# Attention steps and output-projection weight loads at other places among a projection's products

## The chip, the cores and the metric

The kernel runs on one core of one Trainium2 chip. The metric is the device time of one execution, in microseconds (us); the time of a kernel is the median over its runs.

## What is computed

One layer of a hybrid encoder on 512 tokens of width 1024. All 16 attention heads are fed by one input projection, and all are gathered by one output projection into the residual. A gated MLP with a short convolution and a gated per-layer embedding follow; the change does not touch these.

```
hn = rms_norm(h, ln_mix);  z = hn @ w_in
q1, q2, k1, k2, va, qf, kf, vf, fg, qc, kc, vc = split(z)     # all q, k: RMS norm per head
o_a = diff_attention(...)        # A: 4 heads, softmax(q1 k1) - lam * softmax(q2 k2), then a norm
o_b = forgetting_attention(...)  # B: 6 heads, bias from a cumulative log forget gate, causal
o_c = chunk_attention(...)       # C: 6 heads, bias by clipped relative position, causal by chunk
h = h + concat([o_a, o_b, o_c]) @ w_out
h = h + conv_gated_mlp(rms_norm(h, ln_ffn), ...)
h = h + (p @ w_ple_proj) * sigmoid(rms_norm(h, ln_ple) @ w_ple_gate)
```

## The kernel before

Heads are worked on in eight pairs: A0, A1, B0, B1, B2, C0, C1, C2, with two heads (0 and 1) in each. The 512 tokens are four tiles of 128. To keep float32 accuracy, every operand of a product is split into a rounded part `hi` and the rest `lo`, and a product is three matmuls (`mm3`, hi*hi, hi*lo, lo*hi).

The input projection runs part by part (`PARTS`: A0, A0b, A1, A1b, B0, B1, B2, C0, C1, C2; A has two sets of queries and keys, so `A1b` is A1's second). Each part has four units, one for each token tile: `in_unit` accumulates eight steps of three matmuls in a PSUM bank `z` (two buffers) and then evicts it: values `V`, sums of squares `sq` on ACT, their reduction `rs` on DVE, a power on POOL, and the scaled queries and keys `zn` on DVE, after which the bank is free. Each such unit is a slot; slots 4 to 39 are these units, 40 to 47 the units of the output projection's first pass (`out_unit`, names `wo`): two column halves of four token tiles, six steps of three matmuls, over pairs 0 to 5. The second pass, `last_out`, adds pairs 6 and 7 (C1 and C2) when C2 is done and is followed by the FFN.

The attention is cut into steps, generators that are run in between the product steps of a slot:

- `a`, `b` (`qk_cols`): transposes of the queries and keys and their splits; POOL moves the halves to their places (tiles `q_q`, `k_k`, `kl`).
- `s...` (`scores`): for each query tile two matmuls into a bank `s` (two buffers), on DVE the bias and the row's extreme in one instruction that evicts the bank (`CUSTOM_DVE_ANT_0` in the profile), the exponential on ACT, a reciprocal on DVE, the scaling on POOL. In A the second set (`A_1b_s` and the like) is subtracted from the first on DVE.
- `p0`, `p1` (`prob_cols`): transposes of head 0's and head 1's probabilities (`pt`, `ptc`) and their splits.
- `v0`, `v1` (`values`): probabilities times values into the bank `o`, evicted into `oall`.
- `n` (`subln`): A's norm; `fc`: the cumulative gate.

`T` gives for each step a slot and the product step in it from which it may run; `run` takes one attention step after each product step and runs what is left over, in a row, when the slot's products are through. With that TensorE's order is written out by hand. The order on ACT, DVE and POOL is chosen at build time by a planner, and `EARLY` raises a step's priority there. SP's queue issues most DMAs.

Weights are loaded into staging tiles (`_r`, four buffers); ACT copies `hi`, and `lo = raw - hi` is made in one of three ways, chosen by `lo_by` from a pair of counts `"w" + part`: `(a, b)` gives the last `a` of the loads to an accumulating DMA (ACT writes `-raw` rounded into `lo`, and a DMA issued on POOL's queue adds `raw`), the `b` before them to POOL, and the rest to DVE. `wO0` and `wO1` are the output projection's pairs 0 to 5 for the two column halves, `wO6` the four loads of pairs 6 and 7, in the order (6,0), (6,1), (7,0), (7,1). Split weights lie in rings of eight tiles.

Nearly all instructions carry L78 in the profile, the line of the helper that records them, so they are told apart by tile names, with the pair's number left out: `A1b_z` are A1b's products, `C_s` scores of any C pair, `wo` products of the output projection, `wo_l` its `lo` weights, `n_t` and `u` the FFN.

Of the kernel before, what the change touches and what calls it, by code (L numbers as in the profile page):

```python
# [53 lines left out]
def kernel(ctx: ExitStack, tc: tile.TileContext, x, xt0, xt, pt_in, small, g_ffn_in, bias_c,  # L54
# [636 lines left out]
    def at(slot, gen, *args, start=1, early=0):  # L691
        steps.setdefault(slot, []).append((start, early, gen, args))
# [8 lines left out]
    def run(fill, todo):  # L701
# [18 lines left out]

    T = {
# [13 lines left out]
    }  # L735
    EARLY = {"C1s1": 80, "B1v0": 20, "C0s1": 20, "C1p0": 20, "B0p0": 10, "A0b": 10, "B1p1": 20, "A1b": 10,
# [5 lines left out]

    def add(key, gen, *args):
        at(T[key][0], gen, *args, start=T[key][1], early=EARLY.get(key, 0))

# [999 lines left out]
```

## Time and profile before

| | |
|---|---|
| median of 3 runs | 728.63 us (727.79 to 728.96) |
| profiled execution | 727.37 us, span 725.6 us |
| granted TensorE clock, mean | 0.999 |
| TensorE busy | 705.8 us (97%) |
| VectorE (DVE) busy | 556.3 us (77%) |
| ScalarE (ACT) busy | 394.1 us (54%) |
| GpSimd (POOL) busy | 267.3 us (37%) |

The span is that of the trace, from the first to the last instruction; the execution's own time has a little around it. A line of the timeline has a start and a duration in us, the engine, the source line, the operation and its tiles (output <- inputs), and in brackets the idle time before it and what ended that. Matmuls overlap their neighbours, so the distance from one start to the next is what each takes of TensorE.

### The profile page before, as it was taken

The numbers are of one execution on the slowest core, as the hardware profiler recorded it, in microseconds if no ns is written. First come the engines' busy times: TensorE is split into PE (matmuls) and PEld (weight loads), VectorE is DVE, ScalarE is ACT, GpSimd is POOL, SyncE is SP. The second block draws the span as 40 slices with busy tenths as digits, with TensorE's granted clock in tenths as the row PEclk, the third lists the DMA queues.
The fourth block names the chain that finished last, engine by engine and source line by source line (L and its number), as shares of the span: only waits on it lengthen the run. The fifth ranks groups of instructions, "written<-read, shape, count | busy, mean of one in ns | idle before, by whom it ended". The sixth has DMA issues, their size and how long they took to land. (4 is left out here: it accounts for less than half of the span.)

```text
span 725.6 us, 11877 instructions
## 1 busy us (share of the span) xinstructions
PE 705.8 (97%) x4218; PEld 632.3 (87%) x4218; DVE 556.3 (77%) x1091; ACT 394.1 (54%) x745; POOL 267.3 (37%) x355
## 2 busy tenths in 40 slices
PE   9998999999999999999999999999999999999997
PEld 8888989898999887889888899888998888899886
DVE  7678788887878855758879968787898779988552
ACT  6656775865766664565555544543444543544821
POOL 5676676756665640211101144031520004361400
PEclk9999999999999999999999999999999999999999
DMA  9454425514211135564545334552263322122531
GB/s 330 170 139 110 124 59 124 138 30 110 88 53 52 59 66 167 170 208 90 144 138 125 101 97 122 142 156 66 88 178 114 95 87 83 57 73 93 159 126 58
DMA packets 36950, 83.22 MB, mean 115 GB/s; under 512 B 4214, under 2 KB 6262, under 8 KB 36892
## 3 DMA queue, kind: packets, MB, share of 16 engines
q1 hardware_dynamic: 32844, 73.52, 32.4%
q0 software_dynamic: 3760, 8.66, 6.4%
q8 instruction: 33, 0.54, 0.3%
q10 hardware_dynamic: 288, 0.30, 0.1%
q14 instruction: 25, 0.20, 0.1%
HBM read 74.19 MB, written 4.21 MB: 108 GB/s over the span
## 5 line engine op out<-in xcount | busy, mean ns | idle before, releaser
L78 DVE TENSOR_TENSOR w_lo<-w_raw,w_hi 128x768 fp32r<-128x768 f32 (+1 forms) x118 | 114.4, 989 | 20.2 <-ACT w_hi L78 19.6
L78 ACT CAST w_hi<-w_raw 128x768 fp32r<-128x768 f32 (+1 forms) x118 | 89.6, 786 | 70.1 <-POOL w_raw L78 32.0
L78 PE MATMUL u<-Tl,w_hi 128*128 128x512 f32 (+1 forms) x336 | 125.5, 374 | 0.8 <-DVE Tl L78 0.8
L78 PE MATMUL u<-Th,w_hi 128*128 128x512 f32 (+1 forms) x336 | 125.6, 374 | 0.6 <-ACT pps L78 0.6
L78 PE MATMUL u<-Th,w_lo 128*128 128x512 f32 (+1 forms) x336 | 125.3, 373 | 0.0
L78 POOL TENSOR_TENSOR w_raw<-w_raw,w_raw 128x768 f32<-128x768 f32 (+1 forms) x30 | 54.3, 1833 | 145.2 <-DVE w_lo L78 113.8
L78 PEld LDWEIGHTS u<-Tl,w_hi 128*128 128x128 f32 x336 | 63.0, 188 | 13.1 <-DVE Tl L78 1.2
L78 PEld LDWEIGHTS u<-Th,w_hi 128*128 128x128 f32 x336 | 63.0, 188 | 12.9 <-ACT pps L78 1.0
L78 PEld LDWEIGHTS u<-Th,w_lo 128*128 128x128 f32 x336 | 63.0, 188 | 12.5
L78 DVE SCALAR_TENSOR_TENSOR c<-u,cols,c 128x511 f32<-128x511 f32 x76 | 56.6, 746 | 18.6 <-ACT c L78 17.4
L78 POOL DMA_DIRECT2D w_raw<-in_w_up_dram x9 | 7.9, 907 | 100.1 <-DMA w_raw<-in_w_up_dram 93.9
L78 ACT ACTIVATE c<-u,cols 128x512 f32<-128x512 f32 x38 | 29.5, 776 | 22.7 <-PE u L78 22.7
L78 PE MATMUL dn_X<-w_hi,g_ah 128*128 128x256 f32 x144 | 40.7, 282 | 0.3 <-DVE h L78 0.3
L78 PE MATMUL dn_X<-w_lo,g_ah 128*128 128x256 f32 x144 | 40.6, 282 | 0.3 <-DVE w_lo L78 0.3
L78 PE MATMUL dn_X<-w_hi,g_al 128*128 128x256 f32 x144 | 40.5, 281 | 0.0
L78 PE MATMUL B_z<-B_h,Th 128*128 128x384 f32 x96 | 34.5, 360 | 0.6 <-DVE B_zn L78 0.6
L78 PE MATMUL C_z<-C_h,Th 128*128 128x384 f32 x96 | 34.3, 357 | 0.0
L78 PE MATMUL B_z<-B_h,Tl 128*128 128x384 f32 x96 | 32.3, 337 | 0.0
L78 PE MATMUL B_z<-B_l,Th 128*128 128x384 f32 x96 | 32.3, 337 | 0.0
L78 PE MATMUL C_z<-C_h,Tl 128*128 128x384 f32 x96 | 32.3, 336 | 0.0
L78 PE MATMUL C_z<-C_l,Th 128*128 128x384 f32 x96 | 32.3, 336 | 0.0
L78 PEld LDWEIGHTS dn_X<-w_hi,g_ah 128*128 128x128 f32 x144 | 27.1, 188 | 0.9 <-ACT w_hi L78 0.5
(484 smaller groups left out, 2143.8 us busy)
## 6 DMA issues: line engine op xcount, KB each, us to landing
w_raw<-in_w_up_dram SPq DMA_DIRECT2D x50, 384.0 KB, 3.9
w_raw<-in_w_down_dram SPq DMA_DIRECT2D x24, 384.0 KB, 3.1
w_raw<-in_w_up_dram SPq DMA_DIRECT2D x22, 256.0 KB, 3.3
B_r<-in_w_in_dram SPq DMA_DIRECT2D x12, 384.0 KB, 3.1
C_r<-in_w_in_dram SPq DMA_DIRECT2D x12, 384.0 KB, 3.3
wo_r<-in_w_out_dram SPq DMA_DIRECT2D x16, 256.0 KB, 3.0
w_raw<-in_w_ple_gate_dram SPq DMA_DIRECT2D x16, 256.0 KB, 3.0
h<-in_x_dram SPq DMA_DIRECT2D x4, 512.0 KB, 7.7
```

Source lines behind the costliest of these rows:

```text
L78: ins = getattr(self.eng, op)(*a, **k)
```

## The change

Both tables are changed: `T` (places of steps, and the counts for three sets of weights that are used: `wB0a`, and `wO0`, `wO1`, `wO6`) and `EARLY`. On TensorE these steps move: A0's second-head scores, two product steps later, so that the last three follow their slot's products in a row; B0's query and key transposes and A1's first values and second transposes, one or two product steps later; C0's second-head scores and first transposes, one or two earlier; C1's steps one to three later; and C2's scores, transposes and values, by 2 to 8 us later in TensorE's order, the four scores of its second head in a row behind the output tile of slot 43. The last of B0's four `lo` parts goes from an accumulating DMA to DVE. In the output projection, `lo` of pair 5, first half, goes from DVE to POOL; of pairs 0 and 1, second half, from POOL to DVE; of pairs 2 to 5, second half, from accumulating DMAs to POOL; of pair 6, second half, from DVE to POOL; of pair 7 from DVE and POOL to accumulating DMAs.

```diff
     T = {
         "A0a": (6, 2), "A0b": (9, 4), "fc": (11, 0), "A1a": (16, 4), "A1b": (17, 0), "A0s01": (10, 4),
-        "A0s02": (10, 5), "A0p0": (12, 3), "A0s11": (13, 0), "A0v0": (12, 5), "A0s12": (13, 1), "A0p1": (15, 5),
-        "A0v1": (16, 7), "A0n": (17, 0), "A1s01": (18, 2), "A1s02": (18, 5), "A1p0": (20, 5), "A1s11": (20, 6),
-        "A1v0": (22, 6), "A1s12": (21, 3), "A1p1": (23, 1), "A1v1": (24, 7), "A1n": (27, 7), "B0a": (22, 2),
-        "B0s0": (24, 1), "B0s1": (24, 1), "B0p0": (25, 0), "B0v0": (25, 1), "B0p1": (26, 0), "B0v1": (26, 2),
+        "A0s02": (10, 7), "A0p0": (12, 3), "A0s11": (13, 2), "A0v0": (12, 5), "A0s12": (13, 5), "A0p1": (15, 5),
+        "A0v1": (16, 7), "A0n": (17, 1), "A1s01": (18, 2), "A1s02": (18, 4), "A1p0": (20, 5), "A1s11": (20, 6),
+        "A1v0": (23, 0), "A1s12": (21, 3), "A1p1": (23, 1), "A1v1": (24, 5), "A1n": (27, 7), "B0a": (22, 3),
+        "B0s0": (24, 1), "B0s1": (24, 1), "B0p0": (25, 0), "B0v0": (25, 0), "B0p1": (26, 0), "B0v1": (26, 1),
         "B1a": (24, 1), "B1s0": (25, 4), "B1s1": (26, 0), "B1p0": (26, 7), "B1v0": (28, 3), "B1p1": (29, 0),
         "B1v1": (29, 3), "B2a": (28, 4), "B2s0": (29, 4), "B2s1": (30, 4), "B2p0": (30, 6), "B2v0": (32, 0),
-        "B2p1": (32, 1), "B2v1": (33, 3), "C0a": (32, 3), "C0s0": (33, 4), "C0s1": (34, 1), "C0p0": (34, 7),
-        "C0v0": (35, 7), "C0p1": (36, 0), "C0v1": (36, 5), "C1a": (36, 0), "C1s0": (37, 3), "C1s1": (38, 4),
-        "C1p0": (38, 5), "C1v0": (40, 0), "C1p1": (40, 2), "C1v1": (41, 0), "C2a": (40, 3), "C2s0": (41, 3),
-        "C2s1": (42, 0), "C2p0": (42, 1), "C2v0": (43, 7), "C2p1": (44, 0), "C2v1": (45, 4), "wA0b": (4, 2),
-        "wA1a": (0, 0), "wA1b": (1, 0), "wB0a": (1, 0), "wB1a": (2, 0), "wB2a": (2, 0), "wC0a": (1, 1),
-        "wC1a": (1, 1), "wC2a": (0, 1), "wO0": (0, 0), "wO1": (4, 4), "wO6": (0, 1),
+        "B2p1": (32, 1), "B2v1": (33, 3), "C0a": (32, 2), "C0s0": (33, 3), "C0s1": (34, 0), "C0p0": (34, 5),
+        "C0v0": (35, 7), "C0p1": (36, 0), "C0v1": (36, 5), "C1a": (36, 1), "C1s0": (37, 4), "C1s1": (38, 5),
+        "C1p0": (39, 0), "C1v0": (40, 1), "C1p1": (40, 3), "C1v1": (41, 2), "C2a": (40, 3), "C2s0": (42, 2),
+        "C2s1": (43, 7), "C2p0": (43, 7), "C2v0": (44, 3), "C2p1": (44, 7), "C2v1": (46, 3), "wA0b": (0, 2),
+        "wA1a": (0, 0), "wA1b": (1, 0), "wB0a": (0, 0), "wB1a": (2, 0), "wB2a": (2, 0), "wC0a": (1, 1),
+        "wC1a": (1, 1), "wC2a": (0, 1), "wO0": (0, 1), "wO1": (0, 4), "wO6": (2, 1),
     }
...
```

In `EARLY`, `B1v0`, `C0v1`, `B1v1`, `C0s0`, `A0p0` and `B1a` lose their priority, `B0v0` goes from 40 to 10, `C1v1` from 40 to 10, `C1s0` from 40 to 20, and new are `C2v1` 10, `C2v0` 80, `A0s02` 20, `C0v0` 40, `B0s0` 20, `B0p1` 20, `B2v1` 80, `fc` 80 and `C2p0` 80.

More of the change, by code (lines that the diff above doesn't have):

```diff
@@ L722 @@
         "A0a": (6, 2), "A0b": (9, 4), "fc": (11, 0), "A1a": (16, 4), "A1b": (17, 0), "A0s01": (10, 4),
[4 rows of a table removed]
[4 rows of a table added]
         "B1a": (24, 1), "B1s0": (25, 4), "B1s1": (26, 0), "B1p0": (26, 7), "B1v0": (28, 3), "B1p1": (29, 0),
         "B1v1": (29, 3), "B2a": (28, 4), "B2s0": (29, 4), "B2s1": (30, 4), "B2p0": (30, 6), "B2v0": (32, 0),
[6 rows of a table removed]
-    }
-    EARLY = {"C1s1": 80, "B1v0": 20, "C0s1": 20, "C1p0": 20, "B0p0": 10, "A0b": 10, "B1p1": 20, "A1b": 10,
[5 rows of a table removed]
[6 rows of a table added]
+    }
+    EARLY = {"C1s1": 80, "C0s1": 20, "C1p0": 20, "B0p0": 10, "A0b": 10, "B1p1": 20, "A1b": 10, "A1v1": 80,
[5 rows of a table added]
     def add(key, gen, *args):
```

10 rows, old and new, of the table EARLY are left out of this document.

## The prediction

> **What bounds the kernel now.** I read the page first, then TensorE's own waits, then its timeline round each wait, and only then the other engines there.
>
> ```profile
> span 725.6 us, 11877 instructions
> PE 705.8 (97%) x4218; PEld 632.3 (87%) x4218; DVE 556.3 (77%) x1091; ACT 394.1 (54%) x745; POOL 267.3 (37%) x355
> ```
>
> TensorE is busy for 97% of the span. The change adds and removes none of its 4218 products; it only puts some of them elsewhere in its order. The time can therefore move only by TensorE's waits. The columns of the next view are: who waited for whom, us in total, times, longest.
>
> ```profile
> PE A1b_z L78 <- DVE A1b_zn L78: 1.0, 1, 1.0
> PE wo L78 <- DMA wo_l<-wo_r: 0.9, 1, 0.9
> PE C_s L78 <- POOL C_k_k L398: 0.4, 1, 0.4
> ```
>
> I set the PE orders of both programs side by side, step by step. Up to the first scores of A0's second head they are the same, and after the last output product as well. Between them, steps move in four places. The first and the last hold these three waits, so they are all that the change can win. Of the other waits none stands where a step moves. The timeline gives their true size, since a product's end overlaps the next one's start and only distances between starts count:
>
> ```profile
> 76.40 0.28 PE L78 MATMUL A1b_z<-A1b_l,Th 128*128 128x256 f32 x1
> 76.52 0.28 PE L78 MATMUL A1b_z<-A1b_h,Tl 128*128 128x256 f32 x1
> 77.78 0.36 PE L78 MATMUL A1b_z<-A1b_h,Th 128*128 128x256 f32 x1 [0.98 <-DVE A1b_zn L78]
> 252.65 0.39 PE L78 MATMUL wo<-wo_h,Tl 128*128 128x512 f32 x1
> 253.43 0.38 PE L78 MATMUL C_s<-C_k_k,C_q_q 128*128 128x256 f32 x1 [0.40 <-POOL C_k_k L398]
> 272.62 0.39 PE L78 MATMUL wo<-wo_h,Tl 128*128 128x512 f32 x1
> 272.85 0.40 PE L78 MATMUL wo<-wo_h,Th 128*128 128x512 f32 x1
> 274.14 0.50 PE L78 MATMUL wo<-wo_l,Th 128*128 128x512 f32 x1 [0.89 <-DMA wo_l<-wo_r]
> 274.48 0.40 PE L78 MATMUL wo<-wo_h,Tl 128*128 128x512 f32 x1
> ```
>
> A 256-wide product takes 0.12 (76.40 to 76.52) and a 512-wide one 0.23 (272.62 to 272.85). So the first wait costs 1.26 - 0.12 = 1.14, the second 0.78 - 0.23 = 0.55, the third 1.29 - 0.23 = 1.06. The product that resumes is itself followed late (274.14 to 274.48 is 0.34, not 0.23), 0.11 more each time. In all 3.1 us, 0.4% of the time, is the most that can come back.
>
> **A0's second head.** Its scores come two product steps later among A1b's products; the last three now stand in a row behind A1b's second tile. That tile is complete sooner, and the chain that frees its bank is put forward on ACT, DVE and POOL:
>
> ```profile
> 73.19 0.69 DVE L78 CUSTOM_DVE_ANT_0 A_e<-A_s,bias_A 128x512 f32<-128x512 f32 x1
> 74.27 0.67 DVE L78 CUSTOM_DVE_ANT_0 A_3b_e<-A_3b_s,bias_A 128x512 f32<-128x512 f32 x1
> 74.87 0.42 DVE L78 TENSOR_REDUCE A1b_rs<-A1b_sq 128x4 f32<-128x256 f32 x1
> 76.09 1.02 POOL L383 TENSOR_TENSOR A1b_rs<-A1b_rs,nhalf 128x4 f32<-128x4 f32 x1
> 77.15 0.48 DVE L78 SCALAR_TENSOR_TENSOR A1b_zn<-A1b_z,rstd,A1b_rs 128x256 f32<-128x256 f32 x1 [1.15 <-POOL A1b_rs L383]
> ```
>
> Before, the reduce (74.87) stands behind both 512-wide score evictions; after, ahead of them. About 0.8 us earlier it carries its power (1.02) and the scaling (0.48) with it, and the 1.14 + 0.11 wait is covered. But there are only two score banks, and three scores in a row need them at the rate of DVE: an eviction of 0.69, 0.2 longer than two products of 0.23, and its hand-over make TensorE wait an estimated 0.3, twice, with 0.11 each to resume: 0.8. Two more things are added on DVE. The subtraction for B0's last weights, until now an accumulating DMA, and A1b's third scaling, which goes behind two subtractions of B1's weights:
>
> ```profile
> L78 DVE TENSOR_TENSOR B_l<-B_r,B_h x7: 937/950/1399, 59.0 to 106.8; 128x768 fp32r<-128x768 f32 x7
> ```
>
> The first lands where DVE idles before the transposed probabilities are evicted, so of its 0.95 I count next to nothing. The second frees a bank that B0's first tile wants; it is held 2 x 0.95 longer, of which by my reckoning all but 0.4 passes before TensorE comes there. This place sums to -1.25 + 0.8 + 0.4 = -0.05. Ends: -1.25 (no new wait) and +0.6 (the old wait stays half).
>
> **B0, A1, C0 and C1.** These steps move by one product step of B or C (three products) to three of the output projection; A1's second-head eviction and C0's first transposes move with them. In the stretch of the first of them TensorE waits for nothing:
>
> ```profile
> 121.00:132.00 11.00, 11.00 (x72) 10.73 (x71) 9.04 (x18) 7.51 (x15) 8.31 (x12) 1.00 0.23 61
> ```
>
> (Columns: stretch, its length, busy time of PE, PEld, DVE, ACT, POOL, granted clock, DMA share, GB/s.) There is nothing to win; DVE has 2 of 11 us free as cover; without it a step would lose its 0.3 to 0.5 us shift. I take 0, with 0 and +0.5 as ends. `wA0b` is never asked for, as A0's weights are loaded without that table.
>
> **C2 and the output projection's weights.** C2's first scores go 3.5 us later, so the key moves on POOL that held them up are done: -0.55 - 0.11. The `lo` halves of weights 2 to 5 of the second column half come from POOL instead of accumulating DMAs, so the 1.06 + 0.11 wait goes, if POOL is in time.
>
> ```profile
> 241.92 3.05 POOL L149 TENSOR_TENSOR wo_l<-wo_r,wo_h 128x512 fp32r<-128x512 f32 x2 [1.75 <-ACT wo_h L78]
> 253.00:284.40 31.40, 30.11 (x150) 24.74 (x150) 14.96 (x41) 15.57 (x36) 8.08 (x13) 1.00 0.37 86
> ```
>
> Four subtractions of 1.5 us fit well into a POOL that is busy for 8 of 31 us, and ACT loses four negated copies. What two of these cost on POOL earlier, at 241.92, goes to DVE, and one of the first half's goes to POOL in its stead; both have over 4 us until their product. Nothing for that.
>
> Then what comes in. The second head's four scores, spread before among the products, now follow the fourth output tile without a product between them. DVE first has to add that tile:
>
> ```profile
> 266.74 0.40 PE L78 MATMUL wo<-wo_h,Tl 128*128 128x512 f32 x1
> 267.17 0.69 DVE L78 TENSOR_TENSOR h<-h,wo 128x512 f32<-128x512 f32 x1 [2.63 <-PE wo L78]
> 253.97 0.29 DVE L78 CUSTOM_DVE_ANT_0 C_e<-C_s,bias_C 128x128 f32<-128x128 f32 x1 [0.98 <-PE C_s L78]
> 112.69 0.28 PE L78 MATMUL A_0b_s<-kl,A_q_q 128*128 128x256 f32 x1
> 113.27 0.39 PE L78 MATMUL A_s<-A_k_k,A_q_q 128*128 128x256 f32 x1 [0.30 <-DVE A_st L78]
> ```
>
> The add starts 0.2 after the next product does and takes 0.6 until the next instruction starts; the first score's eviction adds 0.3 and frees the bank at 1.15. TensorE wants it after four products of 0.12, at 0.47: 0.7, and 0.11 to resume, +0.8. The nearest row agrees: A1's four scores in a row lose 0.58 - 0.12 at 113.27 alone. Ends 0.5 and 1.3.
>
> ACT's copy for weight 6 now stands ahead of those scores' exponentials, and waits for its load, which waits for a staging tile that POOL frees with its first subtraction:
>
> ```profile
> wo_r<-in_w_out_dram SPq DMA_DIRECT2D x16, 256.0 KB, 3.0
> 272.20 0.62 ACT L78 CAST wo_h<-wo_r 128x512 fp32r<-128x512 f32 x1 [3.10 <-DMA wo_r<-in_w_out_dram]
> ```
>
> Queued behind it are two exponentials, the first head's transposes and weight 6's other half, which waits likewise. Weight 6's first half is so there 1.5 + 3.0 + 0.6 = 5.1 us after its tile's last reader, the other half two subtractions later. Followed through ACT's queue, the second head's last probability is then ready just when its transposes come, an estimate; I count +0.2, ends 0 and +1.5.
>
> Last, both weights 7 get their `lo` halves by accumulating DMA instead of DVE and POOL. Their tiles come free only when the last tile of the first pass has begun:
>
> ```profile
> 284.39 0.40 PE L78 MATMUL wo<-wo_h,Th 128*128 128x512 f32 x1
> 285.34 1.32 ACT L78 CAST wo_h<-wo_r 128x512 fp32r<-128x512 f32 x2 [2.97 <-PE wo L78]
> 263.45 0.64 ACT L78 ACTIVATE wo_l<-wo_r 128x512 fp32r<-128x512 f32 x1
> 264.39 1.90 POOL L142 DMA_DIRECT2D wo_l<-wo_r  x2 [1.26 <-ACT wo_l L78]
> DMA to landing us min/median/max: 3.4/4.5/6.6
> A1b_l<-A1b_r POOLq DMA_DIRECT2D x1, 256.0 KB, 6.4
> 289.53 0.40 PE L78 MATMUL wo<-wo_l,Th 128*128 128x512 f32 x1
> 290.93 0.40 PE L78 MATMUL wo<-wo_l,Th 128*128 128x512 f32 x1
> ```
>
> From 284.39 the `hi` tile takes 0.95, the `lo` tile one product less, 0.7. The negated copy takes 0.64 and the issue follows 0.30 later (263.45 to 264.39): 1.65. The product needs it at 289.53 - 284.39 = 5.14. With a landing of 3.4 it is in time, with 4.5 it is 1.0 late, with the 6.4 of the lone accumulation of this size 2.9. The second is issued at 3.5, behind the first `hi` copy, the copy that splits C2's result (0.62 each) and its own negated one, and is needed at 6.54 plus the first's delay: 0.4 more. That is +0.4, +1.5 or +3.4. I take 0.7, near the short end: 4.5 and 6.6 belong to four that queue, here two go out 1.9 apart. The Trainium skill, "DMA: Bandwidth & Descriptors", section on the anatomy of one DMA on the SWDGE path, gives about 2.0 us fixed plus the bytes at 436 GB/s, an estimate of 2.6 us for 256 KB. By it both land in time and the sum would be 0.7 lower; the rows above (3.4 to 6.6) speak against it.
>
> SP's loads of two projection weights wait for these landings, and the FFN's first weights behind them:
>
> ```profile
> 288.61 4.54 SPq L78 DMA_DIRECT2D w_raw<-in_w_up_dram  x4
> 313.38 0.38 PE L78 MATMUL u<-Th,w_hi 128*128 128x256 f32 x1 [0.55 <-ACT pps L78]
> ```
>
> They are wanted 25 us after 288.61; some 6 us of delay is covered.
>
> **The sum.** -0.05 - 0.66 - 1.17 + 0.8 + 0.2 + 0.7 = -0.2. The profiled execution took 727.37, span 725.6 and 1.77 round it, so 727.2 on that scale; the median of the runs is 728.63, 1.26 above it, which I carry over: 728.4. About 0.2%, 1.46 us, can be told from no change, so this is the same time.
>
> **Rivals.** *The accumulations land in time* (3.4 or less): 0.7 off, 727.7, still the same. For it: SP loads little just then. Against: no row under 3.4. *Faster:* A's scores don't wait because the evictions keep up, so the 1.25 comes back but for 0.25 on a bank, and the DMA is in time: -1.0 - 0.66 - 1.17 + 0.8 = -2.0, 726.6. For it: the loss at 77.78 is one chain's, and the chain is moved forward. Against: evictions of 0.69 against 0.46 of products. *Slower:* the accumulations land like the lone one, 6.4: +3.4 instead of +0.7, so +2.5, 731.1; from 5.4 on it decides. For it: that row, and the loads for the FFN that SP has still to start. That nothing at all changes is excluded by the moved steps, and its time would be the forecast's.
>
> **How the numbers follow.** Forecast 0.33, in time 0.12: both within 0.2%, so same 0.45. Faster 0.32, for the chain is moved forward and all three waits are met. Slower 0.23, from the late landing. The range reaches from a bit below the faster rival (most of the 3.1 us, less the 0.8 that I am surest of) to the late landing: 726.2 to 731.0.
>
> **What would show it.** Right: no wait of A1b products for A1b_zn, none of wo on a DMA near 274, none of C_s on POOL; instead waits of A_s on A_st near 73, of C_s on C_st just before the first head's transposes, and of wo on a DMA into wo_l at the products of weights 7, after the last tile of the first pass. Wrong: a wait of C_pt over 1 us, of wo on a DMA over 2 us, or any new wait between 121 and 250 us.

## The result: 732.76 us, slower by 0.64%

The changed kernel takes 732.76 us (median of six runs, 731.18 to 734.05), the kernel before 728.06 beside it (727.27 to 728.96). The ratio is 1.0064, with a 95% interval of 1.0049 to 1.0079. The profiled execution took 732.71 with a span of 730.9, against 727.37 and 725.6: 5.3 more to explain.

The page's head of the changed kernel:

```profile
span 730.9 us, 11864 instructions
PE 709.1 (97%) x4218; PEld 634.1 (87%) x4218; DVE 557.5 (76%) x1091; ACT 391.6 (54%) x742; POOL 268.2 (37%) x355
```

And those of TensorE's waits in it that bear on the change (who waited for whom, us in total, times, longest):

```profile
PE wo L78 <- DMA wo_l<-wo_r: 3.6, 1, 3.6
PE B_s L78 <- DVE B_st L78: 1.1, 3, 0.6
PE C_s L78 <- DVE C_st L78: 0.5, 1, 0.5
PE B_s L78 <- POOL B_k_k L398: 0.4, 1, 0.4
PE B_z L78 <- DVE A1b_zn L78: 0.2, 1, 0.2
```

The three waits of before that the change was to meet are gone: no `A1b_z` on DVE, no `C_s` on POOL, and the wait of `wo` on a DMA near 274 too. The longest wait is now a new one, 3.6 us on a DMA into `wo_l`. The timeline puts it at the products of weights 7:

```profile
290.05 0.50 PE L78 MATMUL wo<-wo_l,Th 128*128 128x512 f32 x1
291.32 0.39 PE L78 MATMUL wo<-wo_h,Th 128*128 128x512 f32 x1
295.32 0.80 PE L78 MATMUL wo<-wo_l,Th 128*128 128x512 f32 x1 [3.61 <-DMA wo_l<-wo_r]
295.92 0.63 PE L78 MATMUL wo<-wo_h,Tl 128*128 128x512 f32 x1
296.34 0.63 PE L78 MATMUL wo<-wo_h,Th 128*128 128x512 f32 x1
298.05 0.63 PE L78 MATMUL wo<-wo_l,Th 128*128 128x512 f32 x1
298.48 0.44 PE L78 MATMUL wo<-wo_h,Tl 128*128 128x512 f32 x1
298.75 0.39 PE L78 MATMUL wo<-wo_h,Th 128*128 128x512 f32 x1
```

By starts the wait is 4.00 - 0.23 = 3.77 (291.32 to 295.32). The products behind it stand 0.42 apart (295.92 to 296.34) until 298.5, and only then 0.23 again. The next view tells why; its columns are the stretch, its length, busy time of PE, PEld, DVE, ACT and POOL, the granted clock, DMA share and GB/s:

```profile
287.00:291.70 4.70, 4.64 (x19) 3.12 (x17) 3.27 (x5) 2.11 (x5) 1.07 (x2) 1.00 0.85 172
291.70:295.30 3.60, 0.01 (x1) 0.00 (x0) 0.00 (x0) 0.62 (x1) 0.00 (x0) 0.98 0.97 283
295.30:298.60 3.30, 3.28 (x8) 2.63 (x9) 1.29 (x2) 1.91 (x4) 0.05 (x1) 0.51 0.72 281
298.60:302.00 3.40, 3.40 (x16) 2.74 (x15) 2.94 (x5) 1.29 (x2) 1.51 (x3) 1.00 0.00 0
```

The granted clock is 0.51 behind the wait: TensorE idled for 3.6 us and then ran at half speed for 3.3. What leads to the wait, first the timeline of POOL's and SP's issues in the changed kernel, then the landing times in the view of the tile `wo_l`:

```profile
286.30 0.92 POOL L142 DMA_DIRECT2D wo_l<-wo_r  x1 [12.90 <-ACT wo_l L78]
287.85 0.85 POOL L142 DMA_DIRECT2D wo_l<-wo_r  x1 [0.64 <-ACT wo_l L78]
287.82 0.33 SPq L853 DMA_DIRECT2D g_ffn<-in_g_ffn_in_dram  x1
288.20 1.00 SPq L877 DMA_DIRECT2D pin<-in_pt_in_dram  x2
```

```profile
DMA to landing us min/median/max: 3.7/5.6/7.4
```

The two accumulations of weights 7 go out 1.55 us apart. The first lands after 3.7, the second after 7.4. In the moment of the second, SP issues the loads of `g_ffn` (512 KB) and of two `pin` tiles (256 KB each). `g_ffn` lies where `oall` lay, so it has to wait until the last head's output has been split, and C2's later steps have moved that: before, the same issues stood 4.6 us earlier, and no accumulation was near them:

```profile
283.16 0.33 SPq L853 DMA_DIRECT2D g_ffn<-in_g_ffn_in_dram  x1
283.58 0.86 SPq L877 DMA_DIRECT2D pin<-in_pt_in_dram  x2
```

The DMA view by stretches (289.0 to 292.4, then 292.4 to 295.3; packets, MB, share of the 16 engines) shows who gets the engines. q1 is SP's queue, q0 POOL's:

```profile
q1 hardware_dynamic: 216, 0.67, 75.3%
q0 software_dynamic: 32, 0.03, 11.3%
...
q1 hardware_dynamic: 348, 0.63, 58.0%
q0 software_dynamic: 144, 0.26, 49.2%
```

In the first stretch POOL's queue gets nothing but the tail of the first accumulation. In the trace's packet records `g_ffn`'s 128 packets of 4 KB start between 289.35 and 291.98. The second accumulation's first packet starts at 292.50, 4.6 us after its issue, and 84 packets of 2 KB from SP's loads behind `g_ffn` start ahead of it too. From there it shares the engines with SP's loads until 294.84. The Trainium skill, "DMA: Bandwidth & Descriptors", section "Queues, rings and completion order", says that an engine takes turns between queues packet by packet, a packet being several descriptors of one queue that it finishes before it switches. The trace agrees so far as that no data of POOL's queue stands among `g_ffn`'s packets and that both queues move data afterwards. It does not show what one such packet is here, nor whether POOL's descriptors were already there while SP's 84 packets went ahead; so why the second accumulation starts so late stays open in this detail.

### The profile page after: what moved, and what is told of

It reads as the page before. It is cut to its first block, busy times and chain, and to the rows that moved or that the text cites. A ratio compares the mean times of both kernels' runs of the same rounds, so it can differ in the third digit from the quotient of the medians.

```text
span 730.9 us, 11864 instructions
## 1 busy us (share of the span) xinstructions
PE 709.1 (97%) x4218; PEld 634.1 (87%) x4218; DVE 557.5 (76%) x1091; ACT 391.6 (54%) x742; POOL 268.2 (37%) x355
## 5 line engine op out<-in xcount | busy, mean ns | idle before, releaser
L78 PE MATMUL wo<-wo_l,Th 128*128 128x512 f32 x64 | 26.3, 411 | 3.7 <-DMA wo_l<-wo_r 3.6
```

Of the source, the lines that this page charges most:

```text
L78: ins = getattr(self.eng, op)(*a, **k)
```

## The experiments

**Weights 7 back on DVE and POOL (e1).**

```
- "wO6": (2, 1)
+ "wO6": (0, 1)
```

> The changed kernel with one entry of the table set back: wO6 is (0, 1) again, so the lo halves of weights 7 come from DVE and POOL and not from two accumulating DMAs; all steps stay at their new places. Theory: the loss is those two DMAs (a wait of 3.6 us and 0.2 at the products of weights 7, and 1.4 to 1.7 us of half clock right behind it), all else sums to about zero: 732.8 - 5.4 = 727.4 us (726.6 to 728.6), no wait of an output product on a DMA. Rival: the moved steps cost the time themselves and the wait at weights 7 only collects it: another wait takes its place, 731 or more.

Measured 727.32 (726.48 to 729.24), ratio to before 0.9987 [0.9979, 0.9996]. There is no wait of `wo` on a DMA in its trace and the clock stays at full behind 290 us. One entry of the table is worth 5.4 us; the whole loss and a little more hangs on it.

**The same entry alone on the kernel before (e2), C2's steps alone (e11), both alone (e12).** e2 has `wO6` (2, 1), e11 the changed kernel's six C2 steps, e12 both; the rest is the kernel before.

> The kernel before with that one entry changed: wO6 (2, 1), so weights 7 get their lo halves by accumulating DMAs, and all steps stay at their old places. Theory (the DMAs alone are harmless; they collide with 1 MB of loads on SP's queue, g_ffn and two pin tiles, that the later steps of C2 move from 283 to 288 us, on top of the second accumulation): here the loads go out 3 us ahead of the first accumulation, both land in 3.4 to 4.5 us, waits of 0.4 to 1.5 us in sum and no half clock: 728.4 to 729.7. Rival (accumulations of this kind are slow whatever else runs): a wait of 3 us or more at weights 7 and the half clock: 732 to 733.

> The kernel before with the six entries of C2's steps alone changed; every lo half stays where it was, weights 7 on DVE and POOL. Theory: the wait of C_s on POOL goes (-0.66), four scores in a row cost 0.7, the wait on the accumulating DMAs near 274 grows by 0 to 1.5 because C2's transposes no longer lie ahead of it; g_ffn and pin go out late here too but meet no accumulation: 728.3 to 729.9. Rival (the late steps themselves delay the last weights' products and the FFN): 731 or more.

> The kernel before with both of these alone: the six entries of C2's steps and wO6 (2, 1). Theory (neither part is bad alone; together the 1 MB of g_ffn and pin arrives ahead of the second accumulation): a wait of 3 us or more on wo_l at weights 7, half the clock behind it, 4.5 to 5.5 more than e11_before_c2: 733 to 735. Rival (the loss comes with the whole of the moved steps, A0 to C1): as e11_before_c2 and e2_before_w7_dma added up, 729 to 730.5.

Measured: e2 729.05, ratio 1.0008 [0.9995, 1.002]; e11 727.37, 0.9991 [0.9982, 0.9999]; e12 733.16, 1.0074 [1.0061, 1.0088]. In e2 the loads go out at 284.1, the accumulations at 287.0 and 288.0, and both land in 3.3 to 3.9 us, as the view of its tile from 270 us on has it:

```profile
DMA to landing us min/median/max: 3.3/3.6/3.9
```

In e12 loads and accumulation meet again; its timeline, then its windows:

```profile
287.80 0.86 POOL L142 DMA_DIRECT2D wo_l<-wo_r  x1 [0.68 <-ACT wo_l L78]
287.77 0.33 SPq L853 DMA_DIRECT2D g_ffn<-in_g_ffn_in_dram  x1
295.11 0.50 PE L78 MATMUL wo<-wo_l,Th 128*128 128x512 f32 x1 [3.62 <-DMA wo_l<-wo_r]
```

```profile
291.50:295.10 3.60, 0.00 (x0) 0.00 (x0) 0.00 (x0) 0.62 (x1) 0.00 (x0) 1.00 0.99 261
295.10:299.10 4.00, 3.99 (x11) 3.14 (x12) 1.89 (x3) 2.28 (x4) 1.01 (x3) 0.57 0.58 221
```

Neither edit costs anything alone to speak of; the two together cost 5.2 to 5.8 (733.16 less 727.99 of the kernel before beside them, or less 727.37 of e11). That is the loss, made anew from two parts, without A0, the middle steps, or weights 0 to 5. One point of e2's expectation was missed: its trace does have a stretch at half the clock, at 316.88, behind a wait of 1.49 for ACT at the start of the FFN, but none at weights 7. The expectation of e11 was too high by 0.9: I thought that the wait on the accumulations near 274 would grow, and it went away, since the four are issued about 1 us earlier there (263.04 to 266.74, against 264.39 to 267.51) and their products come in another order.

**The loads sent later (e3: `g_ffn` and `pin`; e5: `g_ffn` alone).** A DVE copy of a column of `h` into the tile makes its load wait for the first pass. e3 has one for each of the three tiles, e5 this one alone:

```
+ dve.tensor_copy(out=g_ffn[:, 0:1], in_=h[:, 3, D - 1 : D])
  nc.sync.dma_start(out=g_ffn, in_=g_ffn_in)
```

> The changed kernel with three DVE copies of one column of h added, the result of the first pass's last tile, into g_ffn's tile and both pin tiles ahead of their loads, so that these 1 MB go out about 3.5 us later, at 291.5; weights 7 keep their accumulating DMAs. Theory (collision with these loads): the second accumulation lands within 4.5 us of its issue instead of 7.4, the wait of 3.6 is under 1.2 and the clock stays full: 727.5 to 729.7. Rival (the second accumulation queues behind the first, or POOL is late in making its descriptors): it lands after 7 us as before, 732 to 733.

> The changed kernel with one DVE copy added ahead of g_ffn's load alone, so that its 512 KB go out behind the first pass; the two pin loads (512 KB) stay where they were. Theory (the second accumulation of weights 7 waits for the bytes that SP put ahead of it): half the bytes are gone, 512 KB at the 416 GB/s of that stretch are 1.3 us, so it lands about 6.1 us after its issue, the wait is 2.3 instead of 3.6 and the time 731.5, or 729.9 where the shorter wait leaves the clock at 1.00. Rival (any load in flight at that moment costs the whole delay): 7.4 and 732.8.

e3 took 734.68, ratio 1.0085 [1.0073, 1.0097]; e5 727.34, 0.9991 [0.9982, 1.0]. The landing times, e3's first, then e5's:

```profile
DMA to landing us min/median/max: 3.4/3.4/3.4
```

```profile
DMA to landing us min/median/max: 3.4/3.4/3.5
```

In both, both accumulations land at once and weights 7 wait for nothing, although they still come by DMA. So the collision was right and the rival, one accumulation queueing behind the other or POOL being late by itself, is out. The time of e3 was missed: with `pin` so late, the projection's first products wait 3.4 us for it (timeline), and the clock drops there instead (windows, 0.58 from 298.5 to 306):

```profile
300.28 0.80 PE L78 MATMUL pp<-w_hi,pT_ah 128*128 128x512 f32 x1 [3.38 <-ACT pT_ah L78]
```

```profile
298.50:306.00 7.50, 4.68 (x9) 2.83 (x10) 6.57 (x10) 2.95 (x5) 3.68 (x5) 0.58 0.19 74
```

e5 missed too, to the good side, and was not the test by bytes that I meant: once `g_ffn` no longer heads SP's queue, `pin`, which waits for nothing, goes out at 273 to 276, and `g_ffn` follows at 292.4. All 1 MB is out of the way, not half.

**The wait filled with work (e4).** Fourteen products into a bank that nobody reads, ahead of the one that waits:

> The changed kernel with 14 products of 512 columns added, into a bank that nobody reads, just ahead of the product that waits: 14 x 0.233 = 3.3 us of TensorE work inside the wait. Theory (the 0.43 us spacing of the seven products behind the wait is half the granted clock, which falls because TensorE idled): the granted clock stays 1.00 there, the products stand 0.233 apart, the time is 1.4 to 1.7 lower: 731.2 (730.6 to 732.0). Rival (the products are slow because DMAs and engines load SBUF then): spacing 0.43 as before, 732.8.

Measured 730.73 (730.35 to 731.54), ratio 1.0028 [1.0018, 1.0038]. The wait is as long, but it is busy, and the clock stays, as its windows show:

```profile
291.70:295.30 3.60, 3.53 (x16) 2.61 (x15) 0.69 (x1) 0.62 (x1) 0.00 (x0) 1.00 1.02 281
295.30:298.60 3.30, 3.30 (x15) 2.67 (x15) 2.53 (x4) 1.76 (x3) 0.00 (x0) 1.00 0.79 288
```

DMA traffic is the same as in the changed kernel (281 and 288 GB/s against 283 and 281), so the slow products there were the clock and not traffic. By the medians 2.0 us of the loss was the clock's, or 2.5 with each kernel set against the kernel before beside it (4.7 less 2.2); by the spacing of the products in the trace it was 1.5.

**The smaller terms (e6, e7, e8, e10).** e6, e7 and e8 start from e1. e6 puts the steps of A1, B0, C0 and C1 back, e7 begins C2's second scores earlier (`"C2s1": (43, 3)`), e8 puts A0's second head and B0's `lo` entry back. e10 is the kernel before with `wO0` (0, 1) and `wO1` (0, 4).

> The kernel of e1_w7_engines (weights 7 on DVE and POOL) with the steps of A1, B0, C0 and C1 put back to their old places; A0's second head, C2 and the other lo entries stay changed. From the trace (TensorE is 0.43 us behind at 92 to 122 us and 1.05 behind at 190 to 231): the moves cost 0.6, so 726.7 (726.0 to 727.4), and no wait of B_s behind a B_z product at 136 and 149 us. Rival (the prediction's zero): as e1, 727.3.

> The kernel of e1_w7_engines with the second head's scores of C2 begun four products earlier in the same tile (C2s1 at (43, 3)), so that a step of products lies between them. Theory (four scores in a row are faster than DVE's evictions): the wait of C_s on C_st, 0.68 by starts, goes: 726.6 (726.0 to 727.3). Rival (it moves to C2's transposes, whose probabilities come no sooner): 727.3, with a wait of C_pt of 0.5 or more.

> The kernel of e1_w7_engines with the scores of A0's second head and B0's lo entry back at their old places. Prediction (the old wait of 1.14 + 0.11 returns; 0.8 of waits between scores and 0.4 on a bank go): 727.3 + 0.05, so 727.4 (726.9 to 727.9), and the wait of A1b_z on A1b_zn is back. Rival (the scores in a row cost nothing that was not lost before anyway, so only the old wait returns): 728.2 or more.

> The kernel before with the lo entries of weights 0 to 5 alone changed (wO0 (0, 1), wO1 (0, 4)): POOL makes the lo halves that accumulating DMAs made. Prediction (-1.06 - 0.11 for the wait of an output product on wo_l near 274): 728.3 - 1.2 = 727.1 (726.6 to 727.9). Rival (POOL is late with four subtractions instead, or what waits next takes it): 728.3, with a wait of wo on POOL.

Measured: e6 726.12, ratio 0.9976 [0.9968, 0.9985]; e7 726.81, 0.9984 [0.9973, 0.9995]; e8 727.21, 0.9987 [0.9978, 0.9995]; e10 726.67, 0.9981 [0.9972, 0.9989]. By the runs alone none of e6, e7 and e8 can be told from e1 (0.9987), as the intervals overlap; the traces can tell. In e10 the products from 276 to 312 stand 1.13 earlier than before, those just ahead of the place 0.04 later: 1.17. In e8 the wait of 1.14 on `A1b_zn` is back, as expected. In e7 the scores of C2 no longer wait, 0.68 by starts in e1. Two waits of `B_s` in the timeline of the changed kernel are not in e6:

```profile
135.93 0.47 PE L78 MATMUL B_s<-B_k_k,B_q_q 128*128 128x512 f32 x1 [0.19 <-DVE B_st L78]
148.95 0.39 PE L78 MATMUL B_s<-B_k_k,B_q_q 128*128 128x256 f32 x1 [0.39 <-POOL B_k_k L398]
```

e6's offset to e1 grows by 0.58 round the first of them, at 136, and not any more behind it. The second, on a key move on POOL, does not belong to the moved steps: e1 and e8 do not have it with the new steps, and e2 has it with the old ones (148.02, a wait of 0.42). It comes and goes from execution to execution.

**Both gains together (e9):** e6 with C2's scores spread.

> The kernel of e6_middle_old with C2's second scores spread as in e7_c2_spread: the two edits that each gained, together. Theory (two separate waits): 726.1 - 0.6 = 725.5 (724.8 to 726.3), with neither the waits of B_s on POOL and B_st at 136 and 149 us nor that of C_s on C_st. Rival (the start of the FFN takes it back, since u waits there for ACT): 726.1, and a wait of u on pps longer by as much.

Measured 724.93 (724.43 to 725.55), ratio 0.9956 [0.9944, 0.9968]. It beats the kernel before and the changed one. Its page's head, and its window over the last stretch of attention:

```profile
span 722.8 us, 11864 instructions
```

```profile
260.00:313.00 53.00, 52.20 (x255) 43.01 (x254) 34.68 (x64) 30.11 (x62) 16.51 (x23) 1.00 0.40 130
```

In the last stretch of attention TensorE is busy for 52.20 of 53 us at full clock.

## Why the prediction was wrong

It said 728.4 and the same time; 732.76 lies above its range. The step that failed is the term for weights 7, +0.7: in the trace it measured +5.6 (0.3 at the first accumulation, 3.8 at the second, 1.5 of half clock). It had three faults, the first two in the term, the third in the weight given to its rival.

- *The landing was taken from the wrong neighbours.* I had 3.4, 4.5 and 6.4 and chose the short end because only two accumulations go out. I had moved C2's steps by 2 to 8 us and followed what they compute, but not what their end sets free: the split of the last head's output releases `g_ffn`'s tile, and SP's 1 MB behind it came 4.6 us later, onto the second accumulation. I named "the loads for the FFN that SP has still to start" in the slower rival alone, without asking when they start. Free of them the accumulations land in 3.3 to 3.9 (e2, e3, e5), where my *in time* rival would have held; with them the second takes 7.4, 0.8 more than the longest row I had (6.6).
- *A late landing was priced as the wait alone.* 3.77 of waiting brought another 1.5 of half clock. I counted waits of TensorE as if it resumed at full speed, but for 0.11.
- *The slower rival* had the right mechanism and the right place, with a chance of 0.23; its 731.1 lacked the 1.0 of longer landing and the clock.

The other terms, on the scale of the span:

- *A0's second head*, -0.05: measured -0.08 (TensorE was 0.52 late ahead of the place and 0.44 behind it). The old wait went; in its place the scores lose 0.62 (predicted 0.8) and the bank for `B_z` 0.42 (predicted 0.4). The rows of the changed kernel's timeline, with a 0.17 wait named at the bank, and behind them C2's third score with its neighbours:

```profile
73.32 0.34 PE L78 MATMUL A_2b_s<-kl,A_q_q 128*128 128x384 f32 x1
73.67 0.50 PE L78 MATMUL A_s<-A_k_k,A_q_q 128*128 128x512 f32 x1
74.00 0.40 PE L78 MATMUL A_s<-kl,A_q_q 128*128 128x512 f32 x1
74.47 0.50 PE L78 MATMUL A_3b_s<-A_k_k,A_q_q 128*128 128x512 f32 x1
74.81 0.39 PE L78 MATMUL A_3b_s<-kl,A_q_q 128*128 128x512 f32 x1
82.16 0.41 PE L78 MATMUL B_z<-B_h,Th 128*128 128x384 f32 x1 [0.17 <-DVE A1b_zn L78]
265.66 0.28 PE L78 MATMUL C_s<-kl,C_q_q 128*128 128x256 f32 x1
266.46 0.44 PE L78 MATMUL C_s<-C_k_k,C_q_q 128*128 128x384 f32 x1 [0.52 <-DVE C_st L78]
266.74 0.33 PE L78 MATMUL C_s<-kl,C_q_q 128*128 128x384 f32 x1
```

- *The middle steps*, 0 with +0.5 as the upper end: measured +0.6, but as a sum of three. The moved steps cost 0.4 at 136, where a score waits for its bank on DVE; a mean of 2 in 11 us free on DVE was no cover there. The wait on POOL at 149 adds 0.7, which the moved steps did not cause (e1, e2, e8). And 0.6 comes back at 170, where before waits 0.49 for DVE (`B_q_p` on `B_zn`). That wait is in every trace with the old `EARLY` table and in none with the new one, e6 with the old steps included; so of the three waits "they are all that the change can win" was wrong. Which entry removes it was not tried.
- *C2's four scores in a row*, +0.8: 0.68 at the third score (266.46) and 0.11 to resume, as told.
- *`C_s` on POOL and `wo` on a DMA*, -0.66 and -1.17: both waits gone, the second worth 1.17 by itself (e10).
- *The first 60 us*, not in the sum: +0.5, and not from the change, since no engine's order differs there. TensorE is 0.89 ahead of before at 28 us, then loses 1.66 in a stretch of 3.4 us at 0.50 of the clock at 32 us, which the execution of before does not have, and gets 0.26 back by 60 us. e1, e4, e5, e6, e9 and e11 have such a stretch near there too, the others have none.
- *The start of the FFN*: 0.6 comes back. The first `u` product waits 0.6 longer for ACT than before (1.19 against 0.55), but two waits of `u` on DVE's `Tl`, 0.37 and 0.38 in before, are gone, with the slow starts behind them 1.25 in all.

Summed up: +0.5 - 0.1 + 0.6 - 0.7 (C2 and the output weights before 294) + 0.3 (first accumulation) + 3.8 + 1.5 - 0.6 = +5.3.

## What to carry to other kernels

When steps move, follow not only their own instructions but what their last reader releases: a tile that comes free later sends a load later, and a transfer on another queue may now stand behind it. Cost a wait of TensorE of some 3 us as the wait and the slow products that follow, or fill it with products that nobody reads. And where a term has an end beyond which it decides the sign, ask what else is in flight at that very moment before choosing the near end.

## What the runs showed of the hardware

**The clock.** The trace's record of the granted clock has the two half-clock stretches of the changed kernel at 32.30 and 295.13, each 3.412 us long, and 262.83 apart, 77 times 3.4133. The Trainium skill, "TensorE: Matmul & The Clock Gate", part 1 on the clock gate, says that a free-running window of about 3.4 us decides, and that a window without work halves the clock for the next. The trace agrees on the length, the grid and the half. The stretch that led to the first one was not idle, though. The windows of the changed kernel, then two of before, each kernel's on the grid of its own clock record:

```profile
28.90:32.30 3.40, 1.68 (x11) 1.31 (x12) 3.35 (x11) 2.42 (x6) 2.86 (x3) 1.00 0.00 0
32.30:35.70 3.40, 3.40 (x18) 3.40 (x18) 3.34 (x6) 2.52 (x4) 1.31 (x2) 0.50 0.25 94
```

```profile
27.30:30.70 3.40, 2.68 (x21) 2.25 (x19) 3.32 (x13) 1.49 (x4) 2.82 (x4) 1.00 0.01 2
30.70:34.10 3.40, 2.42 (x19) 2.24 (x20) 3.40 (x9) 3.00 (x5) 1.79 (x2) 1.00 0.00 0
```

TensorE worked for 1.68 of 3.40 us there and the clock still fell; in before the grid cuts the same sparse stretch into windows of 2.68 and 2.42, and the clock stays. The traces of all the kernels agree on where the limit lies: laid on each trace's own grid, every window at full clock with up to 1.78 us of TensorE busy (e1, 30.58 to 33.99) was followed by half the clock, and every one with 1.89 or more (e12, 29.41 to 32.82) by the full clock. So whether a sparse stretch costs clock depends on where the grid falls on it. Little of that reaches the time: of the runs of the kernel before, those with a mean clock of 0.997 or less have median spans 0.1 to 0.6 us above those with 0.999 or more.

**Filling an idle engine pays.** Fourteen products without use made the kernel 2.0 us faster than waiting did (e4).
